# Four fixed PSUM places for group B's chain, and TensorE's written order for a part of the program alone

## The chip, the core and the metric

The kernel runs on one core of a Trainium2 chip. The metric is the device time of one launch in microseconds (us), as a median of several runs. A core has TensorE for matrix products (PE in the profile, its weight loads PEld), VectorE (DVE), ScalarE (ACT), GpSimd (POOL) and SyncE (SP), which issues most transfers. Each engine takes its instructions strictly in their order; between engines, semaphores hold one until another is done. Matrix products land in PSUM, from where VectorE and ScalarE read them.

## The reference, cut to what matters

One layer projects normalised tokens (2048 latent and 256 context tokens, width 1024) into two groups of eight heads. Group A is a gated linear recurrence, group B a gated DeltaNet. Both are scanned forwards and backwards in chunks, and both are joined in an output projection. What the change touches is group B's step from chunk to chunk:

```
def step(s, inp):
    u0_i, w_i, k_dec, d_last = inp[:4]
    v_new = u0_i - jnp.einsum("bhck,bhkv->bhcv", w_i, s)
    s_new = d_last[..., None, None] * s + jnp.einsum("bhck,bhcv->bhkv", k_dec, v_new)
    ...
    q_dec, p_i = inp[4:]
    o = jnp.einsum("bhtk,bhkv->bhtv", q_dec, s) + jnp.einsum("bhts,bhsv->bhtv", p_i, v_new)
    return s_new, o
```

## The kernel before, in words

Tokens are taken in groups of 256 (two chunks of 128), nine groups a head: one of context, eight of latent tokens. A counter T of ticks runs over heads and groups together: in tick T the projections of one group of one head are computed, and beside them run lanes, which are generators that are advanced slot by slot: group A's units, group B's convolutions, keys, values, the inverse of a triangular matrix (`inverse_base`, `inverse_levels`) and two lanes with the chain, one forwards (direction 0) and one backwards (direction 1). A slot holds about half a projection (12 matmuls); `yield 2` in the chain lets two slots pass. Ticks 9 to 17 are the first head's pass, and 80 is the last tick with projections; a drain and the output projection come behind.

A step of the chain (`BHead.chain`, called from `group` and `context`) has four products in one PSUM tile of 128 x 4 x 128 values, one 2 KB bank. `p1` = kT·S and `o1` = qT·S stand behind each other; VectorE makes `r` of p1 (L979); two slots later `p2` = zb·r (L981), of which ScalarE makes `ud` (L984) and `u` (L987); two slots later `p3` = kn·ud (L990) and p1 again = P·u (L993). VectorE then makes the next state S of p3 (L999), and `out` in `group` adds o1 and P·u to the output: in a group's first pass by a ScalarE copy and a VectorE operation (L1089, L1090), in the second by two VectorE operations (L1092, L1093). The tile is taken from a pool with one buffer for each direction, so the next step's p1 has to wait until all of these have read it.

A scheduler builds each engine's order from priorities and its own estimate of times; lanes of the chain have a high priority. TensorE is the exception: a loop at the end of `hybrid_kernel` ties each of its instructions to the one before it, from tick 9 to the end, so TensorE runs them in the order in which the program wrote them:

```
    for i in traced[begun:]:
        if i.engine == mybir.EngineType.PE:
            if prev is not None:
                tc.add_manual_dep(i, prev.name, ...
```

Of the kernel before, what the change touches and what calls it, by code (L numbers as in the profile page):

```python
# [10 lines left out]
F32 = mybir.dt.float32  # L11
# [4 lines left out]
ALU = mybir.AluOpType  # L16
AX = mybir.AxisListType
PSUM = bass.MemoryType.PSUM
DRAM = bass.MemoryType.DRAM

P = 128
# [342 lines left out]
def prep_w(K, cols, places):  # L364

    out = []
    for _ in prep_steps(K, cols, places, out):
        pass
    return out
# [280 lines left out]
class BHead:  # L650
# [308 lines left out]
    def chain(self, d, gi, c, out, last):  # L959


        K, nc, h = self.K, self.K.nc, self.h
        q = self.q[gi]
        s = self.S[d]
        i = gi * GC + c

        def col(t):
            return t[:, d, h, i:i + 1]
        zb = q[f"zb{d}"][:, c, :]
        pc = K.pc.tile([P, 4, P], F32, tag=f"c{d}", name="pc")  # L970
        p1, p2, p3, o1 = (pc[:, j, :] for j in range(4))
        if s is None:
            r = q["v"][:, c, :]
        else:
            nc.tensor.matmul(p1, lhsT=q["kT"][:, c, :], rhs=s, start=True, stop=True)  # L975
            if out is not None:
                nc.tensor.matmul(o1, lhsT=q["qT"][:, c * P:c * P + P], rhs=s, start=True, stop=True)
            r = K.ck.tile([P, P], F32, tag=f"r{d}", name="r")
            nc.vector.scalar_tensor_tensor(r, p1, col(K.neb), q["v"][:, c, :], op0=ALU.mult, op1=ALU.add)  # L979
            yield 2  # L980
        nc.tensor.matmul(p2, lhsT=zb, rhs=r, start=True, stop=True)  # L981
        if not last:
            ud = K.ck.tile([P, P], F32, tag=f"ud{d}", name="ud")
            nc.scalar.activation(ud, p2, AF.Copy, scale=q["rk"][:, 1 + d, c:c + 1])  # L984
        if out is not None:
            u = K.ck.tile([P, P], F32, tag=f"u{d}", name="u")
            nc.scalar.activation(u, p2, AF.Copy, scale=q["rk"][:, 0, c:c + 1])  # L987
        yield 2
        if not last:
            nc.tensor.matmul(p3, lhsT=q["kn"][:, c, :], rhs=ud, start=True, stop=True)  # L990
        if out is not None:

            nc.tensor.matmul(p1, lhsT=q[f"P{d}"][:, c, :], rhs=u, start=True, stop=True)  # L993
        if not last:
            sn = K.ck.tile([P, P], F32, tag=f"S{d}", name="S", bufs=2 + d)
            if s is None:
                nc.vector.tensor_copy(sn, p3)
            else:
                nc.vector.scalar_tensor_tensor(sn, s, col(K.el), p3, op0=ALU.mult, op1=ALU.add)  # L999
            self.S[d] = sn  # L1000
        if out is not None:
            out(c, o1, col(K.neb), p1)

    def masked(self, gi, d):

# [188 lines left out]
def all_heads(K, A, B):  # L1194
# [8 lines left out]
    for T in range(N, N * np_):  # L1203
# [36 lines left out]
        if xa:  # L1240
            (L.u0, L.u1)[o % 2].add(xa.unit(o))
            fa = xa.project(o, hh, vb)
        fb = chain(kb.project(o, "k", hh) if kb else (), vb.project(o, "vq", hh) if vb else ())
        if o == 0 and xa:

# [21 lines left out]
def columns(K):  # L1267

    t = triple(K)
    return t, [[x[:, :, j] for x in t] for j in range(3)]  # L1270


def prepare_early(K, A, B, p):

    a = A.get(p)
    if a:
        _, at = columns(K)
        yield from together([(2, into(K, a, "fb", [COL["af"] + P * a.h, COL["ab"] + P * a.h], at[:2])),
                             (1, into(K, a, "q", [COL["aq"] + P * a.h], at[2:]))])
# [547 lines left out]
EARLY = 4  # L1827
XT = 4


@with_exitstack
def hybrid_kernel(ctx, tc, args, out, heads_a=range(NH), heads_b=range(NH), final=True, dbg=None):
    K = Ctx()
    K.tc, K.nc = tc, tc.nc
    a = args
    K.cp = ctx.enter_context(tc.tile_pool(name="cp", bufs=1))
    K.ws = ctx.enter_context(tc.tile_pool(name="ws", bufs=8))
    K.sm = ctx.enter_context(tc.tile_pool(name="sm", bufs=4))
    K.dr = ctx.enter_context(tc.tile_pool(name="dr", bufs=1, space=DRAM))
    K.drr = ctx.enter_context(tc.tile_pool(name="drr", bufs=2, space=DRAM))  # L1840
    K.w_in = a["w_in"].rearrange("o (k p) n -> p (o k) n", p=P)
    K.y_d = K.dr.tile([SEQ, 2 * D], F32, name="y_d")

    tile_ = dict(reuse_waits="tile")
    right = dict(side="right", reuse_waits="tile")
    cw, cm, cr, ci, co = (ExitStack() for _ in range(5))
    o = Out(K, co, a, out)

    def open_(c, name, bufs, **kw):
        return c.enter_context(tc.tile_pool(name=name, bufs=bufs, **kw))  # L1850

    A = {i + 1: AHead(K, h) for i, h in enumerate(heads_a)}
    B = {i: BHead(K, h) for i, h in enumerate(heads_b)}

    def each(gi, hh):
        x = B.get(0)
        if x:
            if gi == 0:
                x.decay_known = False
                x.w["k"], = prep_w(K, [COL["bk"] + P * x.h], columns(K)[1][:1])  # L1860
            for _ in x.project(gi, "k", hh):
                pass
            for u in {0: (0,), 3: (1,), 5: (2,), 7: (3,), 8: (4,)}.get(gi, ()):
                for _ in x.keys(u):
                    K.used = 0
        if gi == 2:
            for _ in prepare_early(K, A, B, 1):
                pass
        if gi == 5:
            K.done = set("XYZ")  # L1870
            for _ in prepare(K, A, B, 1):
                pass

    K.wp = open_(cw, "wp", W_BUFS // 3)
    K.wr = open_(cw, "wr", 2), "raw"
    K.bp = open_(cw, "bp", 2)
    K.bt = open_(cw, "bt", 1)
    K.hp = open_(cm, "hp", 2)
    K.bk = open_(cm, "bk", 1)
    K.pm = open_(cm, "pm", 2, space=PSUM)  # L1880
    K.ps = open_(cr, "ps", 2, space=PSUM, **right)
    K.lv, K.pq_n, K.used, K.fdone = None, 0, 0, 0
    K.bcon = open_(cr, "bcon", 1, **right)
    K.drg = open_(cr, "drg", 24, space=DRAM)
    K.rt = open_(cr, "rt", 1, **right)
    K.gt = open_(cr, "gt", 2, **right)
    with ExitStack() as c2:
        for _ in setup(K, c2, ExitStack(), a, each):
            K.lv = open_(cr, "pl", 1, space=PSUM, **right).tile([P, 512], F32, name="lv")
            K.psa = open_(cm, "psa", 1, space=PSUM, **tile_)  # L1890
            K.at = open_(cm, "at", 1, **tile_)
    K.pc = open_(cr, "pc", 1, space=PSUM, **right)
    K.ck = open_(cr, "ck", 1, **right)
    K.ho = open_(cr, "ho", 2, **right)
    K.iv = open_(ci, "iv", 1, **right)
    K.d6 = open_(ci, "d6", 2, **right)
    L = K.slots = Slots(K)
    if 0 in B:
        L.dec.add(B[0].all_decays())
        B[0].decay_known = True  # L1900
    traced = K.nc.cur_bb.bb.instructions
    begun = len(traced)

    n = max(len(heads_a), len(heads_b))
    for T in all_heads(K, A, B):
        t = T - N * (n + 1)
        if t == -N:
            L.w.add(w_out_scale(K, a))
        if t == -7 and final:
            L.w.add(o.all_weights(0))  # L1910
        if t == -1 and final:
            L.w.add(o.all_weights(1))
    L.drain(L.u0, L.u1, L.keys, L.dec)
    if final:
        cm.close()
        o.begin()
        xa, xb = A[n], B[n - 1]
        o.ready = lambda i: xb.fdone == NG and max(xa.bdone, xb.bdone) <= i // GC + 1
        for _ in o.tiles():
            if ci and not L.inv.busy() and not L.w.busy():  # L1920
                ci.close()
                ci = None
                L.w.add(o.weights(W_BUFS, 16, o.pool("wo", 1)))
            L.go()
    L.drain(*L.lanes)

    prev = None
    for i in traced[begun:]:
        if i.engine == mybir.EngineType.PE:
            if prev is not None:  # L1930
                tc.add_manual_dep(i, prev.name, mybir.DependencyInfo(
                    mybir.DependencyClass.NoSync, mybir.DependencyReason.DATA), reason="slots")
            prev = i
    co.close()
    if not final:
        cm.close()
        ci.close()
    cw.close()
    cr.close()
    if dbg is not None:  # L1940
        dbg(K)
# [26 lines left out]
```

## Time and profile before

| | |
|---|---|
| median of 3 runs | 3503.6 us (3501.9 to 3505.45) |
| the profiled execution | 3521.75 us, its span 3520.0 us |
| granted TensorE clock, mean | 0.947 |
| busy share of the span | PE 88%, DVE 70%, ACT 52%, POOL 42% |

The profiled execution is one run of its own and stands 0.5% above the median. PE is busy when a matmul is under way; the rest of the span is time in which it waits. The granted clock is the share of full speed: 1 is 2.4 GHz, 0.5 is 1.2 GHz.

### The profile page before, as it was taken

What the parts mean: (1) busy time and instruction counts of PE and PEld (TensorE: products, weight loads), DVE (VectorE), ACT (ScalarE), POOL (GpSimd) and SP (SyncE); (2) the same over time, 40 slices, a digit from 0 to 9 for tenths busy, and PEclk for the clock granted to TensorE, in tenths of its full rate; (3) what the DMA queues carried; (4) which work ended last, traced back from release to release, by engine and by line L of the source; (5) the groups of instructions that cost most, each with busy time, mean ns of one, the idle gap of its engine ahead of it and who ended that gap; (6) DMA issues with size and microseconds to landing.
All of it is one profiled execution on the core that took longest, in us unless ns stands there. A gap on an engine that the chain in (4) does not pass through costs nothing.

```text
span 3520.0 us, 95277 instructions
## 1 busy us (share of the span) xinstructions
PE 3114.7 (88%) x37768; PEld 2428.3 (69%) x37768; DVE 2471.4 (70%) x6600; ACT 1845.0 (52%) x4914; POOL 1490.4 (42%) x2534
## 2 busy tenths in 40 slices
PE   7849898988899889898998989999989799697998
PEld 3637676877787777777777777777778577564554
DVE  5756688677867786788678767877787677654332
ACT  5644455555655555555556555555455655544332
POOL 3523644454436452655255535644444443521000
PEclk9979999999999999999999999999999899898999
DMA  7644334444445544554445444544444653534321
GB/s 246 232 141 126 113 117 132 143 152 150 138 126 158 163 129 132 159 161 136 133 150 167 141 137 140 172 137 131 141 142 132 202 158 118 187 123 156 112 91 54
DMA packets 433875, 508.44 MB, mean 144 GB/s; under 512 B 110740, under 2 KB 336916, under 8 KB 421524
## 3 DMA queue, kind: packets, MB, share of 16 engines
q1 hardware_dynamic: 396308, 477.18, 43.4%
q10 hardware_dynamic: 37120, 25.18, 2.2%
q8 instruction: 296, 4.85, 0.6%
q14 instruction: 151, 1.24, 0.1%
HBM read 346.35 MB, written 155.88 MB: 143 GB/s over the span
## 4 chain that ended last, share of the span: by engine, by line
PE 35%; DVE 21%; DMA 14%; issue 11%; ACT 10%; POOL 8%; SPq 1%; ACTq 0%; POOLq 0%; DVEq 0%
DVE acc L724 5%; PE pm L416 5%; PE pm L417 4%; PE pm L418 4%; DMA df<-dd 3%; PE po L1807 3%; DVE QK L1494 2%; PE pz L407 2%; PE pz L408 2%; PE pz L409 2%; ACT sk L1484 2%; POOL br L850 2%; DMA br<-row_d 2%; DMA raw<-in_w_in_dram 1%; POOL or L58 1%
## 5 line engine op out<-in xcount | busy, mean ns | idle before, releaser
L416 PE MATMUL pm<-h,whi 128*128 128x256 f16 x3256 | 918.0, 282 | 5.3 <-DVE g L1334 4.8
L417 PE MATMUL pm<-h,whi 128*128 128x256 f16 x3256 | 915.1, 281 | 0.0
L418 PE MATMUL pm<-h,wlo 128*128 128x256 f16 x3256 | 914.1, 281 | 0.0
L724 DVE SCALAR_TENSOR_TENSOR acc<-pad,cw,acc 128x504 f32<-128x504 f32 (+1 forms) x768 | 565.4, 755 | 16.9 <-ACT acc L718 11.5
L416 PEld LDWEIGHTS <-whi 128*128 128x128 f16 x3328 | 339.5, 102 | 52.0 <-DVE g L1334 1.0
L418 PEld LDWEIGHTS <-wlo 128*128 128x128 f16 x3328 | 335.9, 101 | 48.7 <-issue 1.2
L417 PEld LDWEIGHTS <-whi 128*128 128x128 f16 x3328 | 335.4, 101 | 48.7 <-issue 5.5
L1484 ACT COPY sk<-QK 128x512 f32<-128x512 f32 x384 | 242.6, 632 | 233.3 <-DVE QK L1494 116.0
L407 PE MATMUL pz<-whi,h 128*128 128x384 f16 (+1 forms) x1152 | 363.5, 320 | 1.0 <-DVE q L1430 0.9
L408 PE MATMUL pz<-wlo,h 128*128 128x384 f16 (+1 forms) x1152 | 362.3, 319 | 0.0
L409 PE MATMUL pz<-whi,h 128*128 128x384 f16 (+1 forms) x1152 | 361.9, 318 | 0.0
L1494 DVE TENSOR_TENSOR QK<-QK,T 128x512 f32<-128x512 f32 x384 | 276.8, 721 | 90.8 <-ACT sk L1484 68.4
L1418 POOL TENSOR_SCALAR QK<-QK,omlb 128x256 f32<-128x256 f32 x144 | 182.1, 1273 | 232.5 <-ACT QK L1414 219.1
L975 PE MATMUL pc<-S,kk 128*128 128x128 f32 x544 | 120.0, 304 | 123.5 <-DVE op L1090 81.3
L850 POOL TENSOR_SCALAR br<-br,nbc 128x128 f32<-128x128 f32 x252 | 179.4, 729 | 66.5 <-DMA br<-row_d 34.0
L975 PEld LDWEIGHTS pc<-S,kk 128*128 128x128 f32 x544 | 89.2, 198 | 154.6 <-DVE op L1090 95.1
L568 POOL TENSOR_TENSOR g<-w,lm 128x128 f32<-128x128 f32 (+2 forms) x120 | 82.1, 684 | 220.1 <-DVE w L618 98.6
L1010 POOL TENSOR_SCALAR_AFFINE_SELECT zb<-zb 128x256 f32<-128x256 f32 x144 | 69.5, 484 | 249.8 <-ACT zb L1015 226.5
L1807 PEld LDWEIGHTS <-yh 128*128 128x128 f16 x1024 | 100.4, 99 | 102.4 <-ACT yh L1790 3.2
L830 ACT ACTIVATE sg<-acc 128x256 f32<-128x256 f32 x208 | 79.5, 412 | 160.7 <-DVE acc L724 133.5
L409 PEld LDWEIGHTS <-h 128*128 128x128 f16 x1152 | 114.6, 99 | 68.5 <-issue 3.2
L984 ACT ACTIVATE ud<-pc,rk 128x128 f32<-128x128 f32 x272 | 99.2, 365 | 115.1 <-PE pc L981 90.3
(363 smaller groups left out, 8110.0 us busy)
## 6 DMA issues: line engine op xcount, KB each, us to landing
h<-hT SPq DMA_DIRECT2D x72, 1024.0 KB
raw<-in_w_in_dram SPq DMA_DIRECT2D x72, 512.0 KB
kk<-kk_d SPq DMA_DIRECT2D x137, 256.0 KB
df<-dd SPq DMA_DIRECT2D x64, 512.0 KB
vq_d<-vq SPq DMA_DIRECT2D x56, 384.0 KB
vq<-vq_d SPq DMA_DIRECT2D x56, 384.0 KB
kk_d<-kk SPq DMA_DIRECT2D x72, 256.0 KB
br<-row_d SPq DMA_DIRECT2D x48, 384.0 KB
```

Of the source, the lines that this page charges most:

```text
L407: nc.tensor.matmul(out, lhsT=h(0, k), rhs=w[0][:, k, :], start=(k == 0), stop=False)
L408: nc.tensor.matmul(out, lhsT=h(0, k), rhs=w[1][:, k, :], start=False, stop=False)
L409: nc.tensor.matmul(out, lhsT=h(1, k), rhs=w[0][:, k, :], start=False, stop=(k == KC - 1))
L416: nc.tensor.matmul(out, lhsT=w[0][:, k, :], rhs=h(0, k), start=(k == 0), stop=False)
L417: nc.tensor.matmul(out, lhsT=w[0][:, k, :], rhs=h(1, k), start=False, stop=False)
L418: nc.tensor.matmul(out, lhsT=w[1][:, k, :], rhs=h(0, k), start=False, stop=(k == KC - 1))
L724: nc.vector.scalar_tensor_tensor(av[:, :, a:b], pad[:, 1 + dy:R + 1 + dy, a + dx:b + dx], wt(dy, dx), av[:, :, a:b], op0=ALU.mult, op1=ALU ...
L850: (nc.vector if h < 1 else nc.gpsimd).tensor_scalar(t[:, c, :], t[:, c, :], K.nbc[:, d, h, b + c:b + c + 1], None, op0=ALU.add)
L975: nc.tensor.matmul(p1, lhsT=q["kT"][:, c, :], rhs=s, start=True, stop=True)
L1484: nc.scalar.copy(view(sk, m, [[-m, 2], [2 * m, 2 * np_], [1, m]]), view(QK, m, [[2 * n - m, 2], [2 * m, 2 * np_], [1, m]]))
L1494: nc.vector.tensor_tensor(qk, qk, view(T, 0, [[nT + 1, 2], [2, 2 * np_], [0, m]]), op=ALU.mult)
L1807: nc.tensor.matmul(po, lhsT=l[:, j, :], rhs=r[k][:, ns], start=f, stop=e)
```

## The change

Each direction gets one PSUM tile for the whole run (`K.pc[d]`) with four places p1, p2, o1 and o2. The product kn·ud goes to p1's place, P·u to o2's. The product o1 = qT·S is written behind u, in the slot of p2, and no longer behind p1. The written order of TensorE is kept only for what is recorded from tick 18 to the end of the ticks; what is recorded earlier, and the drain and output projection behind, are left to the scheduler.

```diff
-        pc = K.pc.tile([P, 4, P], F32, tag=f"c{d}", name="pc")
-        p1, p2, p3, o1 = (pc[:, j, :] for j in range(4))
+        p1, p2, o1, o2 = (K.pc[d][:, j, :] for j in range(4))
         if s is None:
             r = q["v"][:, c, :]
         else:
             nc.tensor.matmul(p1, lhsT=q["kT"][:, c, :], rhs=s, start=True, stop=True)
-            if out is not None:
-                nc.tensor.matmul(o1, lhsT=q["qT"][:, c * P:c * P + P], rhs=s, start=True, stop=True)
             r = K.ck.tile([P, P], F32, tag=f"r{d}", name="r")
...
         if out is not None:
             u = K.ck.tile([P, P], F32, tag=f"u{d}", name="u")
             nc.scalar.activation(u, p2, AF.Copy, scale=q["rk"][:, 0, c:c + 1])
+            nc.tensor.matmul(o1, lhsT=q["qT"][:, c * P:c * P + P], rhs=s, start=True, stop=True)
         yield 2
         if not last:
-            nc.tensor.matmul(p3, lhsT=q["kn"][:, c, :], rhs=ud, start=True, stop=True)
+
+            nc.tensor.matmul(p1, lhsT=q["kn"][:, c, :], rhs=ud, start=True, stop=True)
         if out is not None:
-
-            nc.tensor.matmul(p1, lhsT=q[f"P{d}"][:, c, :], rhs=u, start=True, stop=True)
+            nc.tensor.matmul(o2, lhsT=q[f"P{d}"][:, c, :], rhs=u, start=True, stop=True)
...
-                nc.vector.scalar_tensor_tensor(sn, s, col(K.el), p3, op0=ALU.mult, op1=ALU.add)
+                nc.vector.scalar_tensor_tensor(sn, s, col(K.el), p1, op0=ALU.mult, op1=ALU.add)
...
-            out(c, o1, col(K.neb), p1)
+            out(c, o1, col(K.neb), o2)
...
+FIXED = 18
...
-    K.pc = open_(cr, "pc", 1, space=PSUM, **right)
+    pc = open_(cr, "pc", 1, space=PSUM, **right)
+
+    K.pc = [pc.tile([P, 4, P], F32, name=f"c{d}") for d in range(2)]
...
-    begun = len(traced)
...
+        if T == FIXED:
+            begun = len(traced)
...
+    ended = len(traced)
     L.drain(L.u0, L.u1, L.keys, L.dec)
...
-    for i in traced[begun:]:
+    for i in traced[begun:ended]:
```

The lines of the changed kernel differ by two or three from here on: p1 is L974 there, r L976, p2 L978, ud L981, u L984, o1 L985, kn·ud L989, P·u L991, S L997. Its two tiles are named c_2401 (forwards) and c_2402 (backwards).

The first place is TensorE's queue in the middle of the program, where a step begins: p1 (`<-S,kk`) stands between a projection (pm) and group A's products (kv). Before:

```order
L418 LDWEIGHTS wlo
L418 MATMUL pm<-h,wlo 128x256
L975 MATMUL pc<-S,kk 128x128 [waits DVE_49]
L977 MATMUL pc<-S,vq 128x128
L1543 MATMUL kv<-v,kt 128x128 [waits Activation_49]
L1543 MATMUL kv<-v,kt 128x128 x3
```

And now:

```order
L418 LDWEIGHTS wlo
L418 MATMUL pm<-h,wlo 128x256
L974 MATMUL c_2402<-S,kk 128x128 [waits DVE_49]
L1541 MATMUL kv<-v,kt 128x128 [waits Activation_49]
L1541 MATMUL kv<-v,kt 128x128 x3
```

The product with the queries (`<-S,vq`) has left its place behind p1; the wait for VectorE at p1 is still there.

The second place is the same step further on in TensorE's queue, at p2 (`<-r,zb`), with group A's products (po) and the inverse's first products (lv) behind it. Before:

```order
L981 MATMUL pc<-r,zb 128x128 [waits DVE_49]
L1564 MATMUL po<-v,At 128x128 [waits PE_49]
L1565 MATMUL po<-S,QK 128x128
L1564 MATMUL po<-v,At 128x128
L1565 MATMUL po<-S,QK 128x128 [waits DVE_49]
L584 MATMUL lv<-g,mt 32x32 [waits Activation_49]
```

And now:

```order
L978 MATMUL c_2402<-r,zb 128x128 [waits DVE_49]
L985 MATMUL c_2402<-S,vq 128x128 [waits Activation_49]
L1562 MATMUL po<-v,At 128x128 [waits PE_49]
L1563 MATMUL po<-S,QK 128x128
L1562 MATMUL po<-v,At 128x128
L1563 MATMUL po<-S,QK 128x128 [waits DVE_49]
```

The product with the queries now stands right behind p2, and it waits for ScalarE.

The third place is TensorE's queue early in the first pass, where the keys' transposes (pt), a weight sum (pq) and the gates' products (lv) stand. Before:

```order
L391 MATMUL pq<-sq,ones 128x2 [waits Activation_49]
L391 MATMUL pq<-sq,ones 128x1 [waits Activation_49]
L741 MATMUL pt<-ident,kk 128x128 [waits DVE_49,Pool_49]
L741 MATMUL pt<-ident,kk 128x128
L326 MATMUL lv<-al,up 128x144 [waits DVE_49]
L327 MATMUL lv<-al,ones 128x144
L741 MATMUL pt<-ident,kk 128x128 [waits DVE_49,Pool_49]
```

And now, around the second of these weight sums:

```order
L418 MATMUL pm<-h,wlo 128x256
L416 LDWEIGHTS whi
L416 MATMUL pm<-h,whi 128x256
L391 MATMUL pq<-sq,ones 128x1 [waits Activation_49]
L741 MATMUL pt<-ident,kk 128x128 [waits Pool_49]
L741 MATMUL pt<-ident,kk 128x128
L417 LDWEIGHTS whi
L417 MATMUL pm<-h,whi 128x256
```

The waiting products stood in a row; now projections (pm) of later groups stand between them.

## Rows read from the trace of the kernel before

**Rows 1.** Windows: busy us (x instructions) of each engine, granted clock, DMA share, GB/s.
```profile
160.00:554.00 394.00, 310.40 (x4198) 250.69 (x4199) 266.61 (x689) 192.77 (x454) 159.31 (x258) 0.89 0.42 132
554.00:3030.00 2476.00, 2241.20 (x29911) 1853.75 (x29912) 1888.05 (x5159) 1361.99 (x3856) 1185.41 (x1970) 0.96 0.48 145
3030.00:3520.00 490.00, 435.13 (x2607) 243.73 (x2605) 208.24 (x469) 186.24 (x393) 76.91 (x164) 0.94 0.35 119
```

**Rows 2.** PE's waits, 554 to 3030 us: total us, times, longest us.
```profile
PE pc L975 <- DVE op L1090: 78.8, 43, 4.5
PE pc L975 <- DVE o L1093: 33.4, 26, 2.8
PE sa L1599 <- ACT sk L1484: 26.9, 12, 9.1
...
PE pc L981 <- DVE r L979: 15.7, 13, 2.1
PE pc L990 <- ACT u L987: 11.4, 8, 2.9
```

**Rows 3.** Timeline of a step that ScalarE takes at once (us, duration us).
```profile
1278.36 0.39 PE L981 MATMUL pc<-r,zb 128*128 128x128 f32 x2
1278.79 0.37 ACT L984 ACTIVATE ud<-pc,rk 128x128 f32<-128x128 f32 x1 [0.65 <-PE pc L981]
...
1279.05 0.36 ACT L987 ACTIVATE u<-pc,rk 128x128 f32<-128x128 f32 x1
```

**Rows 4.** Timeline of two steps that find ScalarE held up.
```profile
1221.38 0.39 PE L981 MATMUL pc<-r,zb 128*128 128x128 f32 x2
...
1226.10 0.46 PE L981 MATMUL pc<-r,zb 128*128 128x128 f32 x2 [2.10 <-DVE r L979]
...
1226.63 0.72 ACT L830 ACTIVATE sg<-acc 128x256 f32<-128x256 f32 x2 [8.43 <-DVE acc L724]
...
1229.12 0.37 ACT L987 ACTIVATE u<-pc,rk 128x128 f32<-128x128 f32 x1
...
1230.73 0.36 ACT L987 ACTIVATE u<-pc,rk 128x128 f32<-128x128 f32 x1
```

**Rows 5.** Timeline: p2 and u of the first and last of 204 steps.
```profile
555.82 0.39 PE L981 MATMUL pc<-r,zb 128*128 128x128 f32 x2
...
557.49 0.36 ACT L987 ACTIVATE u<-pc,rk 128x128 f32<-128x128 f32 x1
...
3028.07 0.38 PE L981 MATMUL pc<-r,zb 128*128 128x128 f32 x2
...
3030.83 0.37 ACT L987 ACTIVATE u<-pc,rk 128x128 f32<-128x128 f32 x1
```

**Rows 6.** L999 (S) and L979 (r): idle of DVE before them, us, times.
```profile
L999 DVE SCALAR_TENSOR_TENSOR S<-S,el,pc x256: 326/339/349, 373.2 to 3288.0; 128x128 f32<-128x128 f32 x128
...
  PE pc L993: 55.8, 43
...
  PE pc L977: 37.9, 43
```

**Rows 7.** Timeline around a wait at p1.
```profile
816.50 0.34 DVE L1090 SCALAR_TENSOR_TENSOR op<-pc,neb,op 128x128 f32<-128x128 f32 x1
...
816.90 0.80 PE L975 MATMUL pc<-S,kk 128*128 128x128 f32 x2 [4.54 <-DVE op L1090]
...
818.77 0.42 PE L416 MATMUL pm<-h,whi 128*128 128x256 f16 x1
```

**Rows 8.** PE's waits, 160 to 554 us.
```profile
PE lv L584 <- DMA mt<-mt_d: 20.6, 2, 16.0
PE pq L391 <- ACT wlo L383: 16.2, 2, 14.7
PE pk L807 <- DVE MT L810: 15.2, 3, 10.9
```

**Rows 9.** PE's waits, from 3030 us to the end.
```profile
PE po L1630 <- DMA df<-dd: 20.0, 4, 12.9
```

More of the change, by code (lines that the diff above doesn't have):

```diff
@@ L996, in chain @@
             if s is None:
-                nc.vector.tensor_copy(sn, p3)
+                nc.vector.tensor_copy(sn, p1)
             else:
-                nc.vector.scalar_tensor_tensor(sn, s, col(K.el), p3, op0=ALU.mult, op1=ALU.add)
+                nc.vector.scalar_tensor_tensor(sn, s, col(K.el), p1, op0=ALU.mult, op1=ALU.add)
             self.S[d] = sn
         if out is not None:
-            out(c, o1, col(K.neb), p1)
+            out(c, o1, col(K.neb), o2)
     def masked(self, gi, d):
```

## Prediction

> **What bounds the kernel now.** I read the windows first, then TensorE's waits, then the timeline of single steps of the chain. To cut the windows I counted TensorE's products in the built order against the trace: the first one written in tick 18 runs at 554 us, and the last ones that the written order will still hold run at 3030 us. So the first cut, 160 to 554 us, is the pass that loses its written order; the second, 554 to 3030 us (63 ticks of 39 us), keeps it; the third is the drain and the output projection, which lose it [rows 1].
>
> The reader is to see that TensorE sets the pace in all three. In the middle it is busy for 2241 of 2476 us and no other engine for more than 1888; it idles for 235 us [rows 1]. Most of that hangs on the chain: 112 us before p1 (L975), in 69 waits of 1.6 us each, for the operations that add the output of the step before (L1090, L1093), 16 us before p2 and 11 us before L990 [rows 2]. TensorE's queue is strict, so whatever is added to these waits holds the projections behind it.
>
> **Waits that were to go and don't.** The two places for o1 and o2 look as if p1 had only to wait for S, which is ready earlier than the output. In the built program the count for which p1 (L974) waits is still that of L1088 or L1091, the output of the step before, in 207 steps of 272; before it was so in 203. The trace of before shows why. S (L999) reads p3, which L990 writes, but VectorE was let go by L993, the later product into another place of the same tile; r reads what L975 writes and was let go by L977 [rows 6]. Waits go by the whole tile, a bank, and not by the place in it. I cost this part at nothing, with two small exceptions: r no longer waits for o1, which ends 0.2 us behind p1, and r is late at p2 in 13 waits of 15.7 us in all [rows 2]: I take 5 us off, between 0 and 16.
>
> The Trainium skill speaks against the fixed places here: "PSUM — Partial Sum Buffer", section "PSUM bank collisions raise a hardware error", says to guard PSUM by bank and quadrant, not by address. The rows on S and r agree [rows 6]. By address, p1 would be rid of its 112 us; by bank of nothing.
>
> **What is added.** The same tracking by the whole tile makes o1 wait for u, since u reads p2 in the same tile, and in the built program it does so in all 256 steps. Before, the product that waited for u was L990, two slots (about a whole projection) further on, and even there u was late 8 times, by 11.4 us [rows 2]. Now o1 stands right behind p2 in 220 steps, all that the written order holds. In the other 36 the scheduler puts 5 to 46 products between, so I cost these at nothing; without that cover each would cost what follows.
>
> TensorE must then stand still from the end of p2 to the end of u, and behind it stand group A's products, the projections, and with them ScalarE's evictions of these. The price is a distance that the trace of before has: p2's end to u's end. At its shortest ud starts at once and u overlaps it: 1278.75 to 1279.41, 0.66 us [rows 3]. The hand-over to TensorE adds 0.06, as from L1090's end to L975's start [rows 7]. So the floor is 220 x 0.72 = 158 us. But ScalarE is often behind: 204 steps with both ud and u lie in the middle cut, from 1.64 us at the first to 2.75 at the last [rows 5]; they sum to 420 us (2.06 each), their median is 1.60, 50 are at the floor and 71 are over 1.8. The ceiling is 220 x 2.12 = 466 us.
>
> Between them: ScalarE's delay is paid once, not by each step that finds it. In one place ScalarE stood 8.4 us for VectorE's convolution; two steps waited behind it, 7.7 us and 4.5 us [rows 4]. Had TensorE stopped at the first until 1229.5, the second would have come to a free ScalarE and paid the floor: 8.4 and not 12.2. Going through all stops in order, shortening each by those of the 20 us (half a tick) ahead of it, never below the floor, leaves a mean of 1.6 us. I take 220 x 1.6 = **+352 us**.
>
> **What these stops pay back.** While TensorE stands, VectorE and ScalarE catch up, so the old waits shrink. The same walk over the 235 us of old idle leaves 97, most of it gone at p1 (112 us) and L990. I take **-137 us**; at least -50, if the late output operations come from transfers and not from a backlog, at most -200.
>
> The clock I leave at nothing. In the middle 0.96 is granted [rows 1]; after the 4.5 us stop at p1 the projections ran at the lower level, 0.42 us each against 0.27 [rows 7]. Long stops at p1 go, long stops at o1 come: +-40 us.
>
> **The order that is let go.** In the first pass TensorE idles for 394 - 310 = 84 us [rows 1], and seven waits make 52 of it: the inverse for its transfer, a weight sum for ScalarE, scores for VectorE [rows 8]. None has to do with the projections written behind it, and the new order puts projections between them. What they then run into is VectorE, busy for 267 of 394 us [rows 1]; in 344 us that would be 78%, as in the middle (76%). So **-50 us**, with bounds of 0 (the scheduler's estimate of times is no better than the written order) and -84. In the tail the one big wait is for group A's transfer back, 20 us in 4 [rows 9], behind which output products can now go: **-15 us**, from 0 to -45.
>
> **Sum.** 352 - 137 - 5 - 50 - 15 = +145 us. The profiled execution, 3521.75 us with a span of 3520.0, would become 3667; the median of the runs, 18 us (0.5%) lower, 3649. That is my forecast: **3649 us**, slower by 4%.
>
> **Rivals.**
> - *The stop is cheap and only changes places with old waits.* If TensorE's halts keep ScalarE so far ahead that nearly every step pays the floor, the chain costs 158 - 137 - 5 = +16 us, and the two freed stretches (-65) decide: 3455 us, faster. The point from which it decides is a mean stop of (137 + 5 + 65) / 220 = 0.94 us. For it: the stop comes in every step, some 10 us apart, and each ends with ScalarE caught up. Against it: ScalarE's delays come from VectorE [rows 4], which goes on in its own order whether TensorE stands or not, and only 50 of 204 steps are at the floor today. 0.17.
> - *The delays are paid each time* (+466, and only -50 back, clock +40): +386, 3890 us. Against it the pair in rows 4. 0.07.
> - *The places do what they seem to do*: neither p1 nor o1 waits for another place. Then 112 + 11 + 5 + 65 = -193, some 3310 us. Against it the counts of the built program and rows 6. 0.02.
> - *The freed order is worth nothing, or costs*: 3649 + 65 = 3714 us; within the forecast's own range.
>
> **How the numbers follow.** 0.70 for the forecast, whose own range is 3530 to 3830: below it lies a mean stop of 1.2 us with the first pass at -84, above it one of 1.9 with -70 paid back and the clock against it. With the rivals, and 0.04 for a sum that happens to end near zero, faster by over 0.2% has 0.19, within 0.2% (about what a measurement of this kernel can tell from no change) 0.04, slower 0.77. The range 3480 to 3830 leaves out the dearest case and most of the cheapest.
>
> **What would show it.** In the changed profile TensorE's waits should have a new first row, o1 (L985) for ScalarE's u (L984): some 200 waits, 250 to 400 us in all; the rows on p1 should be there still, but shorter, 20 to 60 us together; the window to tick 18 should be some 50 us shorter. A row at L985 under 200 us would make the forecast too high; if p1's rows vanish, waits go by place and I misread them; if the first pass is not shorter, VectorE or the transfers bound it. The forecast falls altogether if L985 shows no waits.

## The result, and the profile after

The changed kernel takes 3784.26 us (3773.44 to 3789.96), the kernel before 3503.68 us beside it: a ratio of 1.0797, with a 95% interval of 1.0772 to 1.0822. Below, brackets behind a ratio hold such an interval, and each ratio is to runs of the kernel before taken beside it. The change is slower by 281 us, where +145 was forecast. The profiled execution has a span of 3788.3 us, 268 more than before.

The windows of the changed kernel, cut at the same instructions as in [rows 1]: the first product written in tick 18 (now at 524 us, before at 554) and the last p2 under the written order (3311 us, before 3030). Columns as there.

```profile
160.00:524.00 364.00, 316.32 (x4187) 250.98 (x4186) 261.35 (x683) 194.21 (x451) 175.32 (x255) 0.94 0.45 139
524.00:3311.00 2787.00, 2324.98 (x29896) 1894.50 (x29896) 1921.31 (x5161) 1396.80 (x3863) 1152.13 (x1972) 0.94 0.42 130
3311.00:3788.30 477.30, 441.01 (x2608) 249.64 (x2606) 200.55 (x459) 181.98 (x385) 73.69 (x161) 0.95 0.36 120
```

The first pass is 30 us shorter than in [rows 1], the tail 13, the middle 311 longer. In the middle TensorE's idle time went from 235 to 462 us, and its busy time from 2241 to 2325 for the same products, at a granted clock of 0.94 instead of 0.96.

TensorE's waits in that middle, as in [rows 2]:

```profile
PE c L985 <- ACT u L984: 359.8, 217, 6.6
PE c L974 <- DVE op L1088: 60.8, 37, 3.6
PE lv L391 <- ACT wlo L383: 15.8, 9, 4.1
PE c L978 <- DVE r L976: 14.4, 7, 3.7
...
PE c L974 <- DVE o L1091: 0.8, 4, 0.2
```

A new first row holds 360 us, o1 waiting for u, 217 times and 1.66 us each. All other idle time together is 462 - 360 = 102 us, where 235 stood. The waits at p1 went from 112 to 62 us; those for the second pass's output (L1091, before L1093) are as good as gone.

One such halt in the changed kernel's timeline (start us, duration us, idle time before and what ended it):

```profile
1278.12 0.27 PE L417 MATMUL pm<-h,whi 128*128 128x256 f16 x1
...
1278.23 0.27 PE L418 MATMUL pm<-h,wlo 128*128 128x256 f16 x1
...
1278.34 0.39 PE L978 MATMUL c<-r,zb 128*128 128x128 f32 x2
1278.35 1.22 ACT L646 COPY ZZ<-w 64x128 f32<-64x128 f32 x4 [1.47 <-DVE w L618]
...
1279.59 0.47 ACT L686 ACTIVATE pad<-pm,wv 128x256 f32<-128x256 f32 x1
...
1280.21 0.37 ACT L984 ACTIVATE u<-c,rk 128x128 f32<-128x128 f32 x1
...
1280.63 0.49 PE L985 MATMUL c<-S,vq 128*128 128x128 f32 x2 [1.90 <-ACT u L984]
...
1282.17 0.42 PE L417 MATMUL pm<-h,whi 128*128 128x256 f16 x1
...
1282.39 0.42 PE L418 MATMUL pm<-h,wlo 128*128 128x256 f16 x1
```

p2 ends at 1278.73. ScalarE is busy with copies for the inverse and an eviction (a copy out of PSUM) until 1280, then makes ud and u, and TensorE goes on 0.05 us after u's end. Compare [rows 3], the floor, where ScalarE was free. Behind this halt the projections take 0.42 us each and start 0.22 us apart, where they took 0.27 and started 0.11 apart before it: by the trace's record the granted clock is at the lower of its two levels there, 1.2 GHz.

### The profile page after: what moved, and what is told of

Same layout as the page of the kernel before. It is cut to its first block, busy times and chain, and to the rows that moved or that the text cites. A ratio compares the mean times of both kernels' runs of the same rounds, so it can differ in the third digit from the quotient of the medians.

```text
span 3788.3 us, 95397 instructions
## 1 busy us (share of the span) xinstructions
PE 3210.2 (85%) x37768; PEld 2475.8 (65%) x37768; DVE 2497.0 (66%) x6600; ACT 1880.7 (50%) x4919; POOL 1472.5 (39%) x2534
## 5 line engine op out<-in xcount | busy, mean ns | idle before, releaser
L416 PE MATMUL pm<-h,whi 128*128 128x256 f16 x3256 | 928.3, 285 | 5.1 <-ACT QK L1412 4.1
L417 PE MATMUL pm<-h,whi 128*128 128x256 f16 x3256 | 926.4, 285 | 0.0
L418 PE MATMUL pm<-h,wlo 128*128 128x256 f16 x3256 | 925.3, 284 | 0.0
L724 DVE SCALAR_TENSOR_TENSOR acc<-pad,cw,acc 128x504 f32<-128x504 f32 (+1 forms) x768 | 574.6, 763 | 12.3 <-ACT acc L718 3.5
L985 PE MATMUL c<-S,vq 128*128 128x128 f32 x512 | 132.5, 343 | 365.4 <-ACT u L984 365.4
L407 PE MATMUL pz<-whi,h 128*128 128x384 f16 (+1 forms) x1152 | 369.0, 325 | 4.7 <-DVE q L1428 3.5
L409 PE MATMUL pz<-whi,h 128*128 128x384 f16 (+1 forms) x1152 | 367.4, 324 | 0.0
L985 PEld LDWEIGHTS c<-S,vq 128*128 128x128 f32 x512 | 84.0, 204 | 413.0 <-ACT u L984 410.7
L1416 POOL TENSOR_SCALAR QK<-QK,omlb 128x256 f32<-128x256 f32 x144 | 162.5, 1137 | 238.1 <-ACT QK L1412 238.0
L997 DVE SCALAR_TENSOR_TENSOR S<-S,el,c 128x128 f32<-128x128 f32 x256 | 87.7, 342 | 181.3 <-PE c L991 148.7
L981 ACT ACTIVATE ud<-c,rk 128x128 f32<-128x128 f32 x272 | 99.1, 364 | 179.6 <-PE c L978 142.9
L974 PE MATMUL c<-S,kk 128*128 128x128 f32 x544 | 113.7, 291 | 66.9 <-DVE op L1088 60.8
```

Of the source, the lines that this page charges most:

```text
L407: nc.tensor.matmul(out, lhsT=h(0, k), rhs=w[0][:, k, :], start=(k == 0), stop=False)
L409: nc.tensor.matmul(out, lhsT=h(1, k), rhs=w[0][:, k, :], start=False, stop=(k == KC - 1))
L416: nc.tensor.matmul(out, lhsT=w[0][:, k, :], rhs=h(0, k), start=(k == 0), stop=False)
L417: nc.tensor.matmul(out, lhsT=w[0][:, k, :], rhs=h(1, k), start=False, stop=False)
L418: nc.tensor.matmul(out, lhsT=w[1][:, k, :], rhs=h(0, k), start=False, stop=(k == KC - 1))
L724: nc.vector.scalar_tensor_tensor(av[:, :, a:b], pad[:, 1 + dy:R + 1 + dy, a + dx:b + dx], wt(dy, dx), av[:, :, a:b], op0=ALU.mult, op1=ALU ...
```

## Experiments

The first four take the change apart: each part undone or done alone.

**o1 back behind p1.** From the changed kernel:

```diff
             nc.tensor.matmul(p1, lhsT=q["kT"][:, c, :], rhs=s, start=True, stop=True)
+            if out is not None:
+                nc.tensor.matmul(o1, lhsT=q["qT"][:, c * P:c * P + P], rhs=s, start=True, stop=True)
...
             nc.scalar.activation(u, p2, AF.Copy, scale=q["rk"][:, 0, c:c + 1])
-            nc.tensor.matmul(o1, lhsT=q["qT"][:, c * P:c * P + P], rhs=s, start=True, stop=True)
```

> The changed kernel with o1 = qT.S written behind p1 again, as before; the fixed places and the freed order stay. Theory (TensorE's halts at o1 for u, less what they pay back, plus the lower clock they bring, are the whole loss of the middle): L985's waits are gone, the middle gives back all of its +311 us, and what stays is the freed order's -31 and -13, so 3460 us (3440 to 3480). Rival 1 (the four fixed places or the order of VectorE and ScalarE that the scheduler makes with them carry a good part of the loss): 3550 us or more.

Measured: 3470.42 us, ratio to before 0.9911 (0.9884 to 0.9938), within the theory's range. Its middle window and its waits there:

```profile
520.60:2989.50 2468.90, 2231.06 (x29898) 1845.66 (x29898) 1882.61 (x5151) 1361.89 (x3859) 1192.09 (x1970) 0.96 0.47 146
```

```profile
PE c L974 <- DVE op L1089: 78.3, 42, 4.8
PE c L974 <- DVE o L1092: 34.5, 26, 3.3
```

The middle is back at 2469 us (before 2476), with the waits at p1 that stood in [rows 2], to within some 1 us each. One line's place is the whole loss, and more.

**The freed order alone.** The kernel before with the written order cut to the ticks from 18 on:

```diff
-    begun = len(traced)
...
+        if T == 18:
+            begun = len(traced)
...
+    ended = len(traced)
...
-    for i in traced[begun:]:
+    for i in traced[begun:ended]:
```

> The kernel before with nothing but the written order cut to tick 18 to the end of the ticks. Theory: -31 in the first pass and -13 in the tail, nothing in the middle: 3460 us (3440 to 3480), and the same within 0.5% as the run with o1 put back. Rival 1: the two differ by more, by what the fixed places do. Rival 2 (a first pass that ends early is given back in the middle, where the chain's waits set the pace): 3495 us or more.

Measured: 3468.5 us, ratio 0.99 (0.988 to 0.992). Its windows:

```profile
160.00:521.00 361.00, 316.31 (x4199) 250.58 (x4200) 262.02 (x688) 195.96 (x454) 177.92 (x257) 0.94 0.45 140
521.00:2990.20 2469.20, 2236.63 (x29898) 1849.40 (x29898) 1882.44 (x5151) 1362.82 (x3858) 1187.75 (x1970) 0.96 0.47 146
2990.20:3466.50 476.30, 436.89 (x2605) 247.12 (x2603) 209.75 (x469) 183.92 (x391) 75.82 (x164) 0.96 0.36 122
```

Against [rows 1] the first pass gives 33 us, the tail 14, the middle 7. That is more than the medians, which lie 34 us apart, because the profiled execution of before stands 18 us above its median. The run with the fixed places alone (below), which has TensorE's order of before, needs 392, 2464 and 490 us for the three windows: the first pass then gives 31 us, the tail 14, and the middle nothing. What the first pass gains is kept, and this run is the same as the one before it, so the fixed places add nothing to it.

**o1 behind u alone.** The kernel before with the line moved as in the change, everything else as it was (places from the pool, written order throughout).

> The kernel before with nothing but o1 written behind u; places from the pool, written order throughout. Theory: 220 and more halts of 1.7 us, 130 paid back, the clock 0.02 lower: the middle's +311 us, so 3815 us (3780 to 3850). Rival 1 (the halts cost only together with the fixed places or the freed order): 3700 us or less.

Measured: 3854.42 us, ratio 1.1 (1.0964 to 1.1035), just over the range. The waits of the whole span:

```profile
PE pc L986 <- ACT u L985: 397.6, 256, 7.4
PE pc L975 <- DVE op L1089: 57.9, 37, 3.6
```

Now all 256 steps halt, those of the first pass and the tail too; there the freed order had shielded 36 of them.

**The fixed places alone.** The kernel before with one tile a direction:

```diff
-        pc = K.pc.tile([P, 4, P], F32, tag=f"c{d}", name="pc")
-        p1, p2, p3, o1 = (pc[:, j, :] for j in range(4))
+        p1, p2, p3, o1 = (K.pc[d][:, j, :] for j in range(4))
```

> The kernel before with nothing but one fixed tile for each direction (p1, p2, p3, o1 and the order of the products as before). Theory (waits go by the whole tile, so a fixed tile waits as a new one from a pool of one does): no change, 3504 us (3490 to 3515), p1 still with over 100 us of waits for L1090 and L1093. Rival (the places let p1 go before the output operations): the waits at p1 vanish and 3390 to 3420 us.

Measured: 3505.55 us, ratio 1.0005 (0.9991 to 1.0019): no change. Its waits at p1 in the whole span:

```profile
PE c L974 <- DVE op L1089: 83.2, 42, 4.6
PE c L974 <- DVE o L1092: 38.6, 30, 5.0
```

The next three vary the halt.

**One direction only.** The changed kernel, with o1 behind u where d is 0 and behind p1 where d is 1.

> The changed kernel with o1 behind u for the forward direction alone; behind p1 for the backward one. Theory (halts add up, each with its share of low clock): half of the +311 us: 3625 us (3580 to 3670), waits for u of 180 to 230 us, granted clock halfway between 0.941 and 0.958. Rival (each halt only lets ScalarE catch up, so that half as many are longer each, or that the clock falls only when there are many): over 3690 or under 3560 us.

Measured: 3605.79 us, ratio 1.0292 (1.0265 to 1.0319), granted clock 0.952. Middle window, and waits in it:

```profile
525.20:3117.30 2592.10, 2270.27 (x29899) 1868.45 (x29898) 1905.22 (x5146) 1376.32 (x3853) 1165.45 (x1970) 0.95 0.45 139
```

```profile
PE c L988 <- ACT u L986: 176.4, 108, 4.4
PE c L974 <- DVE op L1091: 57.7, 36, 4.1
```

Half the halts are 176 us, 1.63 each: they add up. The loss is a little under half: against the run with o1 put back the middle is 123 us longer, with all halts 318; the medians are 135 and 314 us longer. The first half of the halts already takes p1's waits down from 113 to 73 us; the second half finds little left to pay back.

**One slot between.** The changed kernel with `yield 1`, then o1, then `yield 1`, in place of o1 and `yield 2`.

> The changed kernel with o1 written one slot behind p2. One slot is some 12 projection matmuls, 1.3 us or more of cover, against halts of 1.66 us in the mean and a floor of 0.72. Theory: the halts at the floor vanish, the long ones lose 1.3 to 2 us each: waits for u of 60 to 150 us instead of 360, and 3530 us (3480 to 3600), between the two. Rival (the halts are synchronisation that comes back elsewhere): 3650 us or more.

Measured: 3472.39 us, ratio 0.991 (0.9881 to 0.9939), better than the theory's range. Waits in the middle:

```profile
PE c L987 <- ACT u L984: 75.4, 62, 3.1
PE c L974 <- DVE op L1090: 65.6, 40, 4.7
PE c L974 <- DVE o L1093: 25.8, 12, 4.7
```

The halts fall from 217 to 62, as expected, but what is left costs nothing: p1 has 91 us where 113 stood with o1 put back, and the middle is 2460 us long. One slot, half a projection, was cover enough here.

**Two slots between.** The changed kernel with o1 between kn·ud and P·u.

> The changed kernel with o1 written two slots later, between kn.ud and P.u. It still waits for u (whole tile), but so do its neighbours, and two slots of projections stand ahead. Theory (the loss is that nothing stands between p2 and o1, not the wait itself): the waits for u shrink to some 10 to 20 us, as at L990 before, and 3470 us (3450 to 3490), as with o1 put back. Rival (o1's wait for u, or S and the output coming later, costs wherever it stands): 3520 us or more.

Measured: 3492.03 us, ratio 0.9963 (0.9949 to 0.9977), 2 us above the theory's range. The waits of the whole span, in the slowest of its ten executions (3502.87 us):

```profile
PE c L974 <- DVE op L1088: 80.5, 45, 5.2
PE c L974 <- DVE o L1091: 45.7, 35, 4.5
PE c L978 <- DVE r L976: 33.0, 25, 4.5
PE c L988 <- ACT u L984: 18.6, 17, 3.3
```

The wait for u is covered. But TensorE now waits 33 us at p2 for r, and p1 waits a little longer. Why r comes later in VectorE's order there was not settled.

**The two tiles cut the other way.** As the last, with p1 and p2 of both directions in one tile and o1 and o2 of both in the other:

```diff
-        p1, p2, o1, o2 = (K.pc[d][:, j, :] for j in range(4))
+        p1, p2, o1, o2 = (K.pc[j // 2][:, 2 * d + j % 2, :] for j in range(4))
```

> As the run with o1 two slots later, but the two tiles are cut the other way: one holds p1 and p2 of both directions, the other o1 and o2 of both. In the built program p1 now waits for S, r or u, and no more for the output operations; o1 waits for the other direction's output operations. Theory (waits go by the tile, so p1's 120 us at the output operations are owed to the sharing of one tile): these vanish from p1, some 30 us come back at o1 and at p1 for the other direction, 3390 us (3340 to 3440). Rival (VectorE's lateness is the cause, and TensorE meets it at the next product instead): 3460 us or more.

Measured: 3515.68 us, ratio 1.0026 (1.0013 to 1.0039). The time is the rival's. The waits of the whole span:

```profile
PE lv L391 <- ACT wlo L383: 63.4, 14, 7.2
PE c L978 <- DVE r L976: 50.8, 44, 3.2
PE c L990 <- DVE o L1091: 28.9, 32, 3.2
PE c L974 <- DVE r L976: 28.7, 18, 3.0
...
PE c L988 <- ACT u L984: 27.3, 34, 2.4
PE c L978 <- ACT u L984: 17.3, 20, 2.4
```

p1 no longer waits for the output operations (126 us in the run before this one), so the wait does follow the tile. But the rival's reason, VectorE's lateness met at the next product, is not shown. The two directions now share each tile, and the built program tells which place, so which direction, each of these instructions belongs to. By that count 148 us of TensorE's waits are for an instruction of the other direction, whose result the waiting product does not need: 29 at p2 and 29 at p1 for its r, 26 at o1 for its output, 21 at kn·ud and 17 at p2 for its u, 26 in smaller ones. The theory put these at 30. In the changed kernel no product of the chain waits for the other direction. So the run trades one sharing for another, and a tile that neither other products nor the other direction use was not tried.

The last two take the written order away altogether.

**No written order, o1 behind u; and the same with o1 behind p1.** The loop that ties TensorE's instructions runs over nothing (`traced[ended:ended]`) in the changed kernel and in the one with o1 put back.

> The changed kernel with TensorE left to the scheduler throughout, o1 still behind u. Theory (the halt comes of the written order, which puts o1 right behind p2; left alone the scheduler puts other products between, as in the 36 free steps): waits for u of 30 to 100 us in all instead of 364, and 3480 to 3600 us, depending on what the scheduler's order costs elsewhere. Rival (o1's wait for u costs in any order): waits for u over 200 us and over 3650 us.

> As the run with o1 put back behind p1, with TensorE left to the scheduler throughout. Theory (in the first pass the freed order gave 33 us because products of unlike origin stood in a row; in the middle the written order is already mixed, and its waits are VectorE's lateness): no gain in the middle, 3470 to 3540 us, and the run without written order but with o1 behind u within 1% of it. Rival (the middle has 235 us of idle to fill as well): under 3440 us.

Measured: 3586.58 us, ratio 1.024 (1.022 to 1.026), and 3630.03 us, ratio 1.0374 (1.0339 to 1.0409). In the first, the wait at o1 (in the whole span) and the window between the same two products as above:

```profile
PE c L985 <- ACT u L984: 12.7, 18, 2.8
```

```profile
520.70:3058.40 2537.70, 2360.51 (x29592) 1884.07 (x29590) 1857.11 (x5101) 1331.15 (x3791) 1237.38 (x1942) 0.97 0.45 141
```

The same line behind u costs 13 us when the scheduler places it, less than the 30 to 100 expected, against 360 under the written order: the halt comes of the two together. With o1 put back the theory missed: 3630 is outside 3470 to 3540, and the pair lies 1.2% apart. In the profiled executions that gap is 40 us, and some 32 of it are the clock (0.954 against 0.961 in the mean): TensorE was busy at the lower level for 63 us more, at half speed, and why is open. The freed order idles less in the middle (177 us) yet takes longer; the last section comes back to it.

## Why the forecast was right in kind and half in size

**What added the halts: right, to within 8 us.** The step priced 220 halts at 1.6 us, +352. They came to 360 us in 217, 1.66 each. Putting the line back takes all of them away, moving it alone brings them, and half of them bring 43% of the loss: this cause is shown. The other 36 steps, which the step left at nothing, cost 6 us.

**What pays back: right in sum, less so in place.** 142 us were to come off the old idle time; 235 - 102 = 133 did. p1 lost 50 of its 112 us, a little less than forecast (20 to 60 were to stay, 62 did). Of the rest about half came off waits for ScalarE (L1599 27 us before, 4 now; L990 11 before, 1 now at L989), and the rest is in small waits for VectorE, GpSimd and transfers. The cheap rival needed a mean halt of 0.94 us. It fell because only 64 of the 217 halts were at the floor (up to 0.76 us); the median was 1.30, and 67 were over 1.8.

**The clock: the term that failed.** I left it at nothing, +-40 us, since long stops at p1 would go as others came. They did not go: of 8 stops over 3 us at p1 6 stayed, and 31 came at o1. In the middle TensorE's busy time grew by 2325 - 2241 = 84 us, at a granted clock of 0.94 against 0.96. With o1 put back it is 2231 us, with half the halts 2270, with all 2325, for the same products: it grows with the halts, 0.4 us for each of idle time. The 227 us that the halts net are so dearer by over a third.

Not all of the 84 us are the clock's. By the trace's record of the clock TensorE was busy at the lower level for 174 us of the middle before and for 284 now. Work there goes at half speed, so 110 us more cost 55. The other 29 us stay when the busy time is counted at full speed: 2154 us before, 2154 to 2157 with the order alone, o1 put back, or the places alone, 2167 with half the halts, 2183 with all. No term of the sum had them. A halt parts products that overlapped. Before, the projection behind p2 starts 0.16 us before p2 ends (1278.75 us, [rows 3]):

```profile
1278.59 0.27 PE L416 MATMUL pm<-h,whi 128*128 128x256 f16 x1
```

And o1 takes 0.49 us behind a halt, where p2 takes 0.39 without one. At 0.26 us for each of the 119 more stretches of idle time (284 against 165) that is some 31 us, an estimate.

**The freed order: half right.** The first pass gave 30 us of the 50 (33 alone), the tail 13 of 15. The idle time left in the first pass, 48 of 84 us, is split over many waits, most of them for VectorE, as the step feared.

**The sum.** 360 - 133 + 84 - 30 - 13 = 268 us, the difference of the two spans. Of the 123 us by which the forecast fell short, in spans, 55 are the clock, 29 the lost overlap, 22 the freed order, and 17 the halts and their pay-back. All four lie on the same side.

**The fixed places: right.** Alone they are worth 0.05% (interval -0.09 to 0.19). The Trainium skill's rule ("PSUM — Partial Sum Buffer", section "PSUM bank collisions raise a hardware error") is to guard by bank and quadrant, and not by address. This case's waits agree, since p1's moved only when the tile was cut otherwise; what would happen without the guard no run here shows.

## What to carry to other kernels

Where an engine's order is written by hand, look at what each moved instruction will wait for and what stands between it and that; one slot of other work turned 360 us of halts into 75 that cost nothing. A place of its own within a PSUM tile frees nothing while waits go by the tile, and two chains that share a tile wait for each other. Free a written order where products that wait for unlike things stand in a row (the first pass and the tail here, -1.0%), not where they are already mixed (freed throughout, +2.4% and +3.7%). The fastest versions tried free the order in that part alone, and have o1 at its old place (3469 and 3470 us, without and with the fixed places) or one slot behind u (3472).

## What the runs showed of the hardware that was not expected

Many halts cost more than their idle time: 0.4 us of busy time came with each microsecond of it, in part by the clock, in part by the lost overlap. The clock's part goes with the long ones among them. Stretches of over 3 us in which TensorE idled went from 10 to 40 in the middle, and the clock fell soon behind 34 of these (behind all 10 before); behind the 158 stretches of under 1.5 us it fell 3 times (before, behind 105, 8 times). That was counted in the traces; no run has short halts alone.

Without the written order TensorE is busy for 2361 us between the two marks, where the written order takes 2231 for nearly the same products, and this at a clock of 0.97 against 0.96. Two things change more often there in TensorE's order. fp16 and fp32 products take turns 2811 times, against 1761. And products on TensorE's whole array (128*128) and on parts of it (32*32, 64*64, 128*32) follow each other more often: the part in use changes 1844 times, against 660. The timeline without the written order, of TensorE's products alone, tells which of the two costs:

```profile
1199.59 0.28 PE L417 MATMUL pm<-h,whi 128*128 128x256 f16 x1
1199.80 0.24 PE L617 MATMUL lv<-g,y 32*32 32x32 f32 x2
1199.98 0.28 PE L418 MATMUL pm<-h,wlo 128*128 128x256 f16 x1
1200.10 0.27 PE L416 MATMUL pm<-h,whi 128*128 128x256 f16 x1
...
1202.39 0.27 PE L417 MATMUL pm<-h,whi 128*128 128x256 f16 x1
1202.51 0.39 PE L974 MATMUL c<-S,kk 128*128 128x128 f32 x2
1202.73 0.27 PE L418 MATMUL pm<-h,wlo 128*128 128x256 f16 x1
```

Projections in a row start 0.11 us apart. An fp32 product, which the trace records as two, takes 0.22 us of TensorE's order between two of them when it uses the whole array: 0.11 for each half, so the turns cost nothing. A small one on 32*32 stretches the same step from 0.11 to 0.39 us, though small products in a row start 0.01 us apart. In the median of this run a small product starts 0.21 us behind one on the whole array, and one on the whole array 0.12 us behind a small one, so each change costs some 0.1 us. For 1184 more changes that is about 120 us, most of the 130. What the scheduler's order costs is thus that it scatters the small products between the projections. The other run without the written order agrees: in its whole span the part changes 2092 times, against 885 with o1 put back under the written order, and its busy time counted at full speed is 3170 us, against 2996. This is read from the traces; no run varies it alone.
